# Values in per-head tile order in DRAM, rotary tables one unit earlier, gated output per head: a hybrid attention and retention block on one core

## The chip, the cores and the metric

The kernel runs on one core of a Trainium2 chip. The metric is the device time of one execution in microseconds. Five engines work side by side: TensorE (PE, with its weight loads PEld), VectorE (DVE), ScalarE (ACT), GpSimd (POOL) and SyncE (SP). Each takes its instructions in program order and waits on semaphores. Here SP issues nearly all loads and ACT nearly all stores.

## The reference

One layer over 2048 latent tokens (a grid of 32 rows by 64 columns) and 256 context tokens, width 1024, all in float32:

```
h   = rmsnorm(x) * (1 + scale) + shift          # scale, shift, gate from silu(c) @ w_ada + b_ada
na_q, na_k, na_v, na_g, r_q, r_k, r_v, r_g = split(h @ w_in)      # 8 parts of 512 columns
# group A: 8 heads of 64; each query sees a clamped 8 x 16 window of the grid and all context keys
p    = softmax([q.k_window / 8 + bias, q.k_ctx / 8])
y_na = (p @ [v_window, v_ctx]) * silu(na_g)
# group B: 4 heads of 128; rotary on q and k; retention forward and backward in chunks of 128
y_ret = head_rmsnorm(o_fwd + o_bwd) * silu(r_g)
out  = rmsnorm(x + gate * (concat(y_na, y_ret) @ w_out))
```

## The kernel before

Each float32 operand of a large product is split into a high and a low part, and a product takes three matrix multiplications (high by high, low by high, high by low). The program is one straight list of instructions in four parts.

**Preparation, 0 to 280 us.** The adaLN vectors, the normalised input in blocks of 512 tokens, the projection of the NA keys, the first units of the NA values.

**The job list, to 525 us** (`run_jobs`, L536). Twelve jobs, j0 to j11, each one group of 256 columns of w_in: j0 and j2 the NA values (9 units each, written to `vS`, 4 heads a group), j1 and j3 the retention keys of the context (one unit each), j4 and j6 the NA gates (8 units each, `gS`), j5 and j7 the retention values of the context (one unit each, `rvS`), j8 and j9 the retention gates (8 units each, `ggS`), j10 and j11 the NA queries (8 units each; the last four stand in the attention). A unit is 24 to 48 matrix multiplications into one of six PSUM buffers (`tform` L351, `tokform` L362); then ACT evacuates it (L395 a gate, L459 a retention value), and one unit later ACT's queue stores it (L143). At the start of job j, `next_w` lets ACT split the weights of job j+1 into high (L330) and low (POOL or DVE, L332), and then SP requests the weights of job j+2 (L169) into a ring of four `st` tiles. All of that stands in ACT's one queue: a split, then the job's evacuations.

Hooks hang between the units of j8 to j10. The adaLN gate row is built there: eight rows of `w_ada` come one after the other into one buffer `wraw` (L563, SP), DVE adds each, scaled, to `gacc` (L566), and the next load waits for that; `wo_row` sums `gacc` over the partitions on PE (L573) behind the second unit of j9, and ACT copies it back. Then eight rows of `w_out` go through the same buffer: DVE multiplies by the gate (L577), ACT casts (L581), POOL subtracts (L582), ACT's queue stores the parts to `woS` (L584), and the next row is loaded.

**Attention, 525 to 1085 us.** 128 tiles (8 heads, 4 query row blocks i, 4 column blocks j) run as a software pipeline over PE, DVE, ACT and POOL: scores, minimum, exponent, normalisation, transposes, product with the values (`pv`), combination. The value window of column block j has 24 or 32 columns (`CWIN`), and a row group is four grid rows, so the values of a tile lie on 96 or 128 partitions. `load_v` (L711 to L716) brings one row group with four loads from `vS`, each of 96 or 128 rows of 512 bytes. `combine` writes the head pair's result into one tile of 128 partitions, and after the odd head POOL multiplies it with the gate (L825) and one store follows. Between the tiles' matrix multiplications the fill stream places the remaining projections, among them the retention keys and queries, whose units request their rotary tables (`t0`, two buffers) in their own middle (`mid`, L405 and L435).

**Retention and output, to 1419 us.** Chunk states, retention, output projection, final norm.

The tile framework gives every DMA of SP and ACT one of eight semaphores, and a DMA waits until the one before it on its semaphore has landed, whichever of the two queues that was in. Which one it gets is fixed when the program is built.

Of the kernel before, what the change touches and what calls it, by code (L numbers as in the profile page):

```python
# [18 lines left out]
P = 128  # L19
# [51 lines left out]
]  # L71
RTYPE = [0, 1, 1, 2]
CTYPE = [0, 1, 1, 2]

# [2 lines left out]
def hybrid_kernel(ctx: ExitStack, tc: tile.TileContext, a: dict, out: bass.AP):  # L77
# [4 lines left out]
    qS = [dram.tile([4, P, 2, 512], F32, name=f"qS{t}") for t in range(4)]  # L82
    kS = [dram.tile([P, 2, LT], F32, name=f"kS{t}") for t in range(4)]
    vS = [dram.tile([LT, 4, P], F32, name=f"vS{t}") for t in range(2)]
    gS = [dram.tile([P, L], F32, name=f"gS{t}") for t in range(4)]
    rqS = [dram.tile([P, L], F32, name=f"rqS{r}") for r in range(RH)]
    rkS = [dram.tile([LT, 2 * P], F32, name=f"rkS{r}") for r in range(2)]
# [121 lines left out]
        rbs[i] = r  # L209

    def spread_copy(i):
        rbs[i, 1] = op.tile([P, 2, P], F32, name="t0")
        nc.vector.tensor_copy(rbs[i, 1], rbs[i].unsqueeze(2).to_broadcast([P, 2, P]))

    def spread(*ii):
# [149 lines left out]
                    yield  # L365
        return pm

    def mid(g, n, fn):
        for m in range(KC):
            next(g)  # L370
            if m == n:
                fn()
            yield
        return (yield from g)
# [23 lines left out]

    rot = {}

    def u_rq(w, c0, ct, b):
        def load():
            for key in ("rot_c", "rot_s"):
                rot[key] = op.tile([P, 512], F32, name="t0")
                nc.sync.dma_start(rot[key], a[key][:, b * 512:(b + 1) * 512])  # L405

        g = tform(w, ct, b)
        pm, n, tok = yield from mid(g, 3, load) if ct == 0 else g
        rc, rs = rot["rot_c"], rot["rot_s"]
# [20 lines left out]
        store(dstt[(c0 % 512) // WG][tp * 256:(tp + 1) * 256, :].rearrange("(t p) d -> p t d", p=P), r, n)  # L430

    def u_rk(w, c0, tp):
        def load():
            rot["k"] = op.tile([P, 2, 2, P], F32, name="t0")
            nc.sync.dma_start(rot["k"], a["rot_k"][tp * 256:(tp + 1) * 256].rearrange("(t p) s d -> p t s d", p=P))  # L435

        g = tokform(w, tp)
        pm = yield from mid(g, 2, load) if tp < 8 else g
        rt = rot.get("k")
# [88 lines left out]
    env["queue"] = nc.scalar  # L528
    spill = [(b, hl, k) for b in (2, 3) for hl in range(2) for k in range(0, KC, 2)]

    def spill_step():
        if spill:
            b, hl, k = spill.pop(0)
            nc.sync.dma_start(hS[b - 2][hl][:, k * 512:(k + 2) * 512], f(blk[b][hl])[:, k:k + 2, :].rearrange("p k t -> p (k t)"))

    def run_jobs(jobs, w, hooks):  # L536
        for j, (c0, units) in enumerate(jobs):
            last = j + 1 == len(jobs)
            wn = next_w(not last)
# [87 lines left out]
    def fill_stream(w):  # L627
# [63 lines left out]
    def load_head(h):  # L691
# [6 lines left out]
        return dict(k2=k2, vh=vh, vc=vc, vt={}, q={})  # L698

    def load_e(hd, h):  # L700
        hd["e"] = kp.tile([P, 16, 32], F32, name="rpbe", bufs=1)
# [9 lines left out]
    def load_v(hd, gs):  # L711
        for g in gs:
            vt = kp.tile([P, 4, P], F32R, name="vt", bufs=6)
            src = hd["vh"][4 * g * GW:(4 * g + 4) * GW, :].rearrange("(r c) d -> r c d", c=GW)
            for j, (c0, cw) in enumerate(CWIN):
                nc.sync.dma_start(f(vt)[:4 * cw, j, :], src[:, c0:c0 + cw, :])  # L716
            hd["vt"][g] = vt

    mrow = mp.tile([P, 3, 16], F32, name="mrow")
# [70 lines left out]
    def pv(t):  # L790
        h, i, j, kr0, kr, kc0, cw = dims(t)
        T, hd = tl_st[t], heads[h]
        pt, ng_, cn = T["pt"], T["ng"], 4 * cw
        if t % 2 == 0:
            tl_st["po"] = psc.tile([P, 2, 2, P], F32, name="po")
        po = tl_st["po"]
        for g in range(ng_):
            nc.tensor.matmul(po[:, t % 2, :, :], hd["vt"][kr0 // 4 + g][:cn, j, :], pt[:cn, g, :, :], start=(g == 0), stop=False)  # L798
# [4 lines left out]
    gts = {}  # L803

    def load_gate(t):
        h, i = dims(t)[:2]
        gts[t // 4] = ap_.tile([P, 512], F32, name="gt", bufs=1)
        nc.sync.dma_start(gts[t // 4], gS[h // 2][:, i * 512:(i + 1) * 512])

    def combine(t):  # L810
        h, i, j = dims(t)[:3]
        po, jp = tl_st["po"], j // 2
        fin = slice(0, 64) if h % 2 == 0 else slice(64, 128)
        oth = slice(64, 128) if h % 2 == 0 else slice(0, 64)
        if h % 2 == 0 and jp == 0:
            ys[i] = ap_.tile([P, 512], F32, name="y2", bufs=4)
# [3 lines left out]
        yv = ys[i][fin].rearrange("p (r w c) -> p w r c", r=8, w=4)[:, 2 * jp:2 * jp + 2]  # L820
        nc.vector.tensor_tensor(yv, po[fin, :, 1, :].rearrange("p j (r c) -> p j r c", r=8),
                                tmp[fin].rearrange("p j (r c) -> p j r c", r=8), ALU.add)
        if h % 2 == 1 and jp == 1:
            gt, y2 = gts.pop(t // 4), ys[i]
            nc.gpsimd.tensor_tensor(y2, y2, gt, ALU.mult)  # L825
            y_put(h // 2, i // 2, (i % 2) * 512, y2, 2)

    def run(n):
        for un in qu[n:n + 1]:
# [127 lines left out]
    for t in range(NT + 3):  # L957
# [391 lines left out]
```

## Time and profile before

| what | value |
|---|---|
| median of 3 runs | 1419.95 us (1419.73 to 1425.41) |
| the profiled execution | 1420.85 us, span 1419.1 us |
| PE busy | 1351.0 us, 95% of the span |
| mean granted TensorE clock | 0.986 |
| value loads (L716) | 256, of 64 or 48 KB |
| DMA traffic | 253.19 MB, mean 178 GB/s |

The span is the time from the first to the last instruction in the trace. A group's row gives busy time, mean length, and the idle time of the engine ahead of it with what ended it. A row of the timeline gives start, length, engine, line, operation, and in brackets the idle time ahead and its releaser. SPq and ACTq are the two engines' DMA issues.

### The profile page before, as it was taken

The numbers are of one execution on the slowest core, as the hardware profiler recorded it, in microseconds if no ns is written. First come the engines' busy times: TensorE is split into PE (matmuls) and PEld (weight loads), VectorE is DVE, ScalarE is ACT, GpSimd is POOL, SyncE is SP. The second block draws the span as 40 slices with busy tenths as digits, with TensorE's granted clock in tenths as the row PEclk, the third lists the DMA queues.
The fourth block names the chain that finished last, engine by engine and source line by source line (L and its number), as shares of the span: only waits on it lengthen the run. The fifth ranks groups of instructions, "written<-read, shape, count | busy, mean of one in ns | idle before, by whom it ended". The sixth has DMA issues, their size and how long they took to land.

```text
span 1419.1 us, 22560 instructions
## 1 busy us (share of the span) xinstructions
PE 1351.0 (95%) x8380; PEld 1181.2 (83%) x8380; DVE 641.2 (45%) x1244; ACT 530.7 (37%) x1155; POOL 560.1 (39%) x579
## 2 busy tenths in 40 slices
PE   6989999999999999999999998898999989999997
PEld 2567899988887887998799888797999879888886
DVE  5786111100021221467766766575663634345445
ACT  5454212212212221555455444354562234333332
POOL 4442302112201221565655644375453155454442
PEclk9999999999999999999999999999999999999999
DMA  9444656223254676556666685757346998555433
GB/s 318 158 164 143 215 207 230 104 97 105 96 157 159 195 276 202 127 156 166 180 157 162 182 243 190 200 153 181 108 125 208 283 297 260 191 170 173 154 120 126
DMA packets 203631, 253.19 MB, mean 178 GB/s; under 512 B 13057, under 2 KB 151425, under 8 KB 202498
## 3 DMA queue, kind: packets, MB, share of 16 engines
q1 hardware_dynamic: 168098, 186.98, 45.2%
q10 hardware_dynamic: 35424, 64.76, 12.5%
q8 instruction: 67, 1.10, 0.3%
q14 instruction: 42, 0.34, 0.1%
HBM read 168.86 MB, written 82.84 MB: 177 GB/s over the span
## 4 chain that ended last, share of the span: by engine, by line
PE 73%; DMA 9%; DVE 6%; issue 3%; POOL 3%; ACT 2%; SPq 2%; DVEq 0%; POOLq 0%; ACTq 0%
PE mm L351 25%; PE mm L362 18%; PE mm L1192 11%; PE sS L751 3%; PE tr L778 2%; PE po L798 2%; PE mm L915 2%; DMA k<-kS 2%; PE tr L780 1%; DMA q<-qS 1%; PE po L800 1%; PE mm L295 1%; PE mm L1104 1%; PE mm L1103 1%; PE mm L1102 1%
## 5 line engine op out<-in xcount | busy, mean ns | idle before, releaser
L351 PE MATMUL mm<-hhi,whi 128*128 128x512 f32 x640 | 260.5, 407 | 0.0
L351 PE MATMUL mm<-hlo,whi 128*128 128x512 f32 x640 | 254.2, 397 | 4.8 <-DVE hlo L264 1.9
L351 PE MATMUL mm<-hhi,wlo 128*128 128x512 f32 x640 | 254.4, 397 | 0.2 <-DVE wlo L332 0.2
L362 PE MATMUL mm<-whi,hhi 128*128 128x256 f32 x768 | 225.5, 294 | 0.0
L362 PE MATMUL mm<-wlo,hhi 128*128 128x256 f32 x768 | 217.7, 283 | 2.5 <-POOL wlo L332 2.5
L362 PE MATMUL mm<-whi,hlo 128*128 128x256 f32 x768 | 217.2, 283 | 0.0
L332 POOL TENSOR_TENSOR wlo<-st,whi 128x256 fp32r<-128x256 f32 (+1 forms) x97 | 111.7, 1171 | 232.7 <-ACT whi L330 232.2
L782 ACT CAST pt<-tr 128x640 fp32r<-128x640 f32 (+1 forms) x128 | 95.6, 747 | 205.4 <-PE tr L780 193.0
L788 DVE TENSOR_TENSOR pt<-tr,pt 128x640 fp32r<-128x640 f32 (+1 forms) x128 | 113.9, 890 | 102.8 <-ACT pt L782 102.1
L362 PEld LDWEIGHTS mm<-wlo,hhi 128*128 128x128 f32 x768 | 146.0, 190 | 3.2 <-POOL wlo L332 3.1
L351 PEld LDWEIGHTS mm<-hlo,whi 128*128 128x128 f32 x640 | 121.4, 190 | 30.1 <-issue 2.5
L362 PEld LDWEIGHTS mm<-whi,hhi 128*128 128x128 f32 x768 | 146.3, 190 | 0.0
L362 PEld LDWEIGHTS mm<-whi,hlo 128*128 128x128 f32 x768 | 146.2, 190 | 0.0
L351 PEld LDWEIGHTS mm<-hhi,wlo 128*128 128x128 f32 x640 | 121.0, 189 | 29.4 <-DVE wlo L332 0.6
L351 PEld LDWEIGHTS mm<-hhi,whi 128*128 128x128 f32 x640 | 121.3, 190 | 28.7 <-issue 4.6
L771 POOL TENSOR_SCALAR sp<-sp,stt 128x640 f32<-128x640 f32 (+2 forms) x128 | 103.4, 809 | 100.7 <-DVE stt L770 79.8
L760 DVE CUSTOM_DVE_ANT_0 sp<-sS,nb 128x640 f32<-128x640 f32 (+2 forms) x128 | 105.5, 825 | 26.4 <-PE sS L751 20.3
L765 ACT ACTIVATE sp<-sp,stt 128x640 f32<-128x640 f32 (+2 forms) x128 | 107.4, 839 | 26.5 <-DVE stt L760 26.0
L751 PE MATMUL sS<-k,q 128*128 128x256 f32 (+3 forms) x512 | 100.6, 319 | 16.9 <-DVE stt L760 13.0
L751 PEld LDWEIGHTS sS<-k,q 128*128 128x128 f32 x512 | 84.5, 191 | 24.4 <-DVE stt L760 15.9
L1192 PE MATMUL mm<-wor,y 128*128 128x512 f32 x384 | 95.4, 397 | 1.0 <-DVE xt L1201 0.9
L1192 PE MATMUL mm<-won,y 128*128 128x512 f32 x336 | 89.9, 406 | 0.0
(216 smaller groups left out, 2307.5 us busy)
## 6 DMA issues: line engine op xcount, KB each, us to landing
st<-in_w_in_dram SPq DMA_DIRECT2D x48, 512.0 KB
q<-qS SPq DMA_DIRECT2D x64, 256.0 KB
vS<-o ACTq DMA_DIRECT2D x18, 512.0 KB
k<-kS SPq DMA_DIRECT2D x16, 576.0 KB
kS<-o SPq DMA_DIRECT2D x16, 512.0 KB
woS<-g ACTq DMA_DIRECT2D x32, 256.0 KB
qS<-o ACTq DMA_DIRECT2D x16, 512.0 KB
vt<-vS SPq DMA_DIRECT2D x128, 64.0 KB
```

The costliest lines, as they stand in the source:

```text
L332: eng.tensor_tensor(l, r, f(h), ALU.subtract)
L351: nc.tensor.matmul(pm[:, :n], ww[:, k, cs], h[:, k, :], start=(k == 0 and i == 0), stop=(k == KC - 1 and i == 2))
L362: nc.tensor.matmul(pm[:, t * WG:(t + 1) * WG], h[:, k, o:o + P], ww[:, k, :], start=(k == 0 and i == 0), stop=(k == KC - 1 and i == 2))
L751: nc.tensor.matmul(o, hd["q"][i][:, hl, j * P:(j + 1) * P], k, start=(hl == 0), stop=(hl == 1))
L760: nc.vector.tensor_tensor_reduce(T["sp"][:, :n], T["s"], nbz[big][:, o:o + n], 1.0, 3e38, ALU.add, ALU.min, T["st"][:, 0:1])
L765: nc.scalar.activation(sp[:, :n], sp[:, :n], AF.Exp, bias=st[:, 0:1], scale=-1.0, accum_out=st[:, 1:2])
L771: nc.gpsimd.tensor_scalar(sp[:, :n], sp[:, :n], st[:, 2:3], 0.0, ALU.mult, ALU.add)
L778: nc.tensor.transpose(tr[:cn, g, :], sp[:, T["lo"] + g * cn:T["lo"] + (g + 1) * cn], ident)
L782: nc.scalar.copy(pt[:, :ng_ + 2, 0, :], tr[:, :ng_ + 2, :])
L788: nc.vector.tensor_tensor(pt[:, :n, 1, :], tr[:, :n, :], f(pt)[:, :n, 0, :], ALU.subtract)
L798: nc.tensor.matmul(po[:, t % 2, :, :], hd["vt"][kr0 // 4 + g][:cn, j, :], pt[:cn, g, :, :], start=(g == 0), stop=False)
L1192: nc.tensor.matmul(pm, yy[:, k, :], ww[:, k, sl], start=(k == 0 and i == 0), stop=(k == 3 and i == 2))
```

## The change

Four edits:

1. A new DRAM tile `vB` per head holds the values in the order in which attention's tiles read them: [row in the tile, row group, window, feature]. 256 copies from `vS` to `vB`, DRAM to DRAM, of 64 or 48 KB (four grid rows by 24 or 32 columns by 512 bytes), are issued on SP, six behind each unit of jobs j4 and on.
2. `load_v` takes two loads per row group from `vB`, of 128 and 96 rows of 1 KB. The windows' order in the tile is `VORD`. Row groups 3 and 4 are requested one tile earlier.
3. The rotary tables are requested in the middle of the unit ahead, from three `t0` buffers; `mid` goes.
4. Gate, product and store run per head on 64 partitions, with two buffers each for gate and result: 32 products on POOL and 32 stores in place of 16.

```diff
+VORD = [1, 2, 0, 3]
...
+    vB = [dram.tile([P, 8, 4, P], F32, name=f"vB{h}") for h in range(NH)]
...
+    def rot_load(key, n):
+        rot[key, n] = t = op.tile([P, 512], F32, name="t0", bufs=3)
+        if key == "rot_k":
+            nc.sync.dma_start(t.rearrange("p (t s d) -> p t s d", t=2, s=2),
+                              a[key][n * 256:(n + 1) * 256].rearrange("(t p) s d -> p t s d", p=P))
+        else:
+            nc.sync.dma_start(t, a[key][:, n * 512:(n + 1) * 512])
+
     def u_rq(w, c0, ct, b):
-        def load():
-            for key in ("rot_c", "rot_s"):
-                rot[key] = op.tile([P, 512], F32, name="t0")
-                nc.sync.dma_start(rot[key], a[key][:, b * 512:(b + 1) * 512])
-
-        g = tform(w, ct, b)
-        pm, n, tok = yield from mid(g, 3, load) if ct == 0 else g
-        rc, rs = rot["rot_c"], rot["rot_s"]
+        pm, n, tok = yield from tform(w, ct, b)
+        rc, rs = rot["rot_c", b], rot["rot_s", b]
...
+    vfmt = []
+    for h in range(NH):
+        vg = vS[h // 4][:L, h % 4, :].rearrange("(r c) d -> r c d", c=GW)
+        for e, j in enumerate(VORD):
+            c0, cw = CWIN[j]
+            for g in range(8):
+                vfmt.append((vB[h][:4 * cw, g, e, :].rearrange("(r c) d -> r c d", c=cw), vg[4 * g:4 * g + 4, c0:c0 + cw, :]))
...
                 tick()
                 spill_step()
+                for _ in range(6 if j > 3 else 0):
+                    if vfmt:
+                        nc.sync.dma_start(*vfmt.pop(0))
                 if hooks.get(j):
                     hooks[j].pop(0)()
...
         def steps(g):
-            for v in g:
+            n = at[0]
+            at[0] += 1
+            short = n > 0 and order[n - 1][0] is u_rq
+            if short:
+                for e in needs(n)[1:]:
+                    rot_load(*e)
+            held = order[n][0] is u_rq
+            for m, v in enumerate(g):
+                if m == 2:
+                    nxt = needs(n + 1)
+                    for e in nxt[:1] if held else nxt:
+                        rot_load(*e)
                 if chop:
                     chop.pop(0)()
                 yield v
...
     def load_v(hd, gs):
         for g in gs:
             vt = kp.tile([P, 4, P], F32R, name="vt", bufs=6)
-            src = hd["vh"][4 * g * GW:(4 * g + 4) * GW, :].rearrange("(r c) d -> r c d", c=GW)
-            for j, (c0, cw) in enumerate(CWIN):
-                nc.sync.dma_start(f(vt)[:4 * cw, j, :], src[:, c0:c0 + cw, :])
+            for e, n in ((0, P), (2, 96)):
+                nc.sync.dma_start(f(vt)[:n, e:e + 2, :], hd["vb"][:n, g, e:e + 2, :])
...
-        if h % 2 == 1 and jp == 1:
-            gt, y2 = gts.pop(t // 4), ys[i]
-            nc.gpsimd.tensor_tensor(y2, y2, gt, ALU.mult)
-            y_put(h // 2, i // 2, (i % 2) * 512, y2, 2)
+        if jp == 1:
+            gt = gts.pop(t // 4)
+            nc.gpsimd.tensor_tensor(y2[fin], y2[fin], gt[fin], ALU.mult)
+            store(yS[i // 2][h // 2, fin, (i % 2) * 512:(i % 2) * 512 + 512], y2[fin], 2)
...
-        if h % 2 == 1 and j == 3:
+        if j == 1:
             load_gate(t)
...
-        for g in {(0, 3): (3,), (1, 0): (4,), (1, 1): (5,), (1, 3): (6,), (2, 3): (7,)}.get((i, j), ()):
+        for g in {(0, 2): (3,), (0, 3): (4,), (1, 1): (5,), (1, 3): (6,), (2, 3): (7,)}.get((i, j), ()):
             load_v(hd, (g,))
```

PE and DVE run the same instructions in the same order as before. SP's order changes at three places.

SP in j4 to j9 of the changed program (L546 the copies, L171 the weights' loads, L565 the loads of the gate chain's rows), rows alike in a run put together:

```order
L546 DMA vB_67<-vS_65 128x1x128 x16
L546 DMA vB_67<-vS_65 96x1x128 x16
L546 DMA vB_68<-vS_65 128x1x128 x16
L171 DMA st<-in_w_in_dram 128x4x256 x2
L546 DMA vB_68<-vS_65 96x1x128 x6
L171 DMA st<-in_w_in_dram 128x4x256 x2
L546 DMA vB_68<-vS_65 96x1x128 x10
L546 DMA vB_69<-vS_65 128x1x128 x16
L546 DMA vB_69<-vS_65 96x1x128 x16
L546 DMA vB_70<-vS_65 128x1x128 x6
L171 DMA st<-in_w_in_dram 128x4x256 x2
```

In the program before these weights' loads follow each other with nothing between. Now j4's 48 copies stand ahead of the weights of j7 (the first row of L171), six more ahead of those of j8, and j6's 48 ahead of those of j9. The 16th copy of j4 has its semaphore from the store of j5's unit (`rvS0<-o`), the ninth of j6 from the store of j7's unit (`rvS1<-o`).

ACT at the start of j6 in the changed program (L450 and L145 j5's evacuation and store, L332 the split of j7's weights, L389 and L145 the first evacuations and stores of j6):

```order
L450 COPY o_2742<-mm_2693 128x512 [waits DMAHW4_49,PE_49]
L145 DMA rvS0_85<-o_2742 128x2x256 [waits Activation_49]
L332 CAST whi_2751<-st_2689 128x1024 [waits DMAHW1_49,Pool_49]
L332 CAST whi_2751<-st_2691 128x1024 [waits DMAHW2_49]
L389 ACTIVATE o_2786<-mm_2761 128x512 [waits DMAHW6_49,PE_49]
L145 DMA gS2_77<-o_2786 128x512 [waits DMAHW4_49,Activation_49]
```

ACT's order is that of before; what moved is the load of `st_2689`, which now stands behind 48 copies on SP, the sixteenth of which waits for the second row here.

SP at the gate chain, before:

```order
L169 DMA st_2993<-in_w_in_dram 128x4x256 [waits DMAHW3_49,DMAHW0_49,Pool_49]
L558 DMA gacc_3027<-in_b_gate_dram 1x1024 [waits DMAHW2_49,DVE_49]
L563 DMA wraw_3030<-in_w_ada_dram 128x1024 [waits DMAHW3_49]
L563 DMA wraw_3061<-in_w_ada_dram 128x1024 [waits DMAHW5_49,DMAHW3_49,DVE_49]
L563 DMA wraw_3092<-in_w_ada_dram 128x1024 [waits DMAHW7_49,DMAHW5_49,DVE_49]
```

and in the changed program:

```order
L560 DMA gacc_3149<-in_b_gate_dram 1x1024 [waits DMAHW6_49,DVE_49]
L565 DMA wraw_3152<-in_w_ada_dram 128x1024 [waits DMAHW7_49]
L546 DMA vB3_70<-vS0_65 96x1x128 [waits DMAHW0_49]
L546 DMA vB3_70<-vS0_65 96x1x128 [waits DMAHW1_49]
L546 DMA vB3_70<-vS0_65 96x1x128 [waits DMAHW2_49]
L546 DMA vB3_70<-vS0_65 96x1x128 [waits DMAHW3_49]
L546 DMA vB3_70<-vS0_65 96x1x128 [waits DMAHW4_49]
L546 DMA vB3_70<-vS0_65 96x1x128 [waits DMAHW5_49]
L565 DMA wraw_3189<-in_w_ada_dram 128x1024 [waits DMAHW7_49,DMAHW6_49,DVE_49]
```

Six copies stand between every two loads of the chain. The first load's semaphore (DMAHW7) was last given to the store of j9's unit 0, `ggS2<-o_3448`, and that of the copy behind it (DMAHW0) to the store of j9's unit 1, `ggS2<-o_3485`; the unit that needs the sum of all eight rows, `wo_row`, stands behind unit 1 on PE.

More of the change, by code (lines that the diff above doesn't have):

```diff
@@ L211, in spread_copy @@
     def spread_copy(i):
-        rbs[i, 1] = op.tile([P, 2, P], F32, name="t0")
+        rbs[i, 1] = op.tile([P, 2, P], F32, name="t0", bufs=3)
         nc.vector.tensor_copy(rbs[i, 1], rbs[i].unsqueeze(2).to_broadcast([P, 2, P]))
@@ L366, in tokform @@
         return pm
[L368 to L374, printed above, removed]
     def u_k(w, c0, ct, b):
@@ L432, in u_rk @@
     def u_rk(w, c0, tp):
[L433 to L439, printed above, removed]
+        pm = yield from tokform(w, tp)
+        rt = rot["rot_k", tp].rearrange("p (t s d) -> p t s d", t=2, s=2) if tp < 8 else None
         o = op.tile([P, 2, 2, WG], F32, name="o")
@@ L642, in next_c, with needs @@
             return w
-        def steps(g):
-            for v in g:
+        order = [(kind, *a_) for kind, c0 in fseq[:4] for b in range(2) for a_ in units(kind, b)]
+        order += [(kind, *a_) for b in range(4) for kind, c0 in fseq[4:6] for a_ in units(kind, b)]
+        order += [(kind, *a_) for kind, c0 in fseq[6:] for b in (2, 3) for a_ in units(kind, b)]
+        at = [0]
+        def needs(n):
+            kind, *a_ = order[n] if n < len(order) else (None,)
+            if kind is u_rk:
+                return [("rot_k", a_[0])]
+            if kind is u_rq and a_[0] == 0:
+                return [("rot_c", a_[1]), ("rot_s", a_[1])]
+            return []
+        def steps(g):
+            n = at[0]
[10 more added lines that the diff above has]
+                        rot_load(*e)
                 if chop:
@@ L697, in load_head @@
         nc.sync.dma_start(f(vc), vh[L:, :].rearrange("(n p) d -> p n d", p=P))
-        return dict(k2=k2, vh=vh, vc=vc, vt={}, q={})
+        return dict(k2=k2, vb=vB[h], vc=vc, vt={}, q={})
     def load_e(hd, h):
@@ L792, in pv @@
         T, hd = tl_st[t], heads[h]
-        pt, ng_, cn = T["pt"], T["ng"], 4 * cw
+        pt, ng_ = T["pt"], T["ng"]
         if t % 2 == 0:
@@ L796, in pv @@
         po = tl_st["po"]
+        cn = 4 * cw
         for g in range(ng_):
-            nc.tensor.matmul(po[:, t % 2, :, :], hd["vt"][kr0 // 4 + g][:cn, j, :], pt[:cn, g, :, :], start=(g == 0), stop=False)
+            nc.tensor.matmul(po[:, t % 2, :, :], hd["vt"][kr0 // 4 + g][:cn, VORD.index(j), :], pt[:cn, g, :, :], start=(g == 0), stop=False)
         for g in range(2):
@@ L803, in hybrid_kernel, with fin_ @@
     gts = {}
+    def fin_(h):
+        return slice(0, 64) if h % 2 == 0 else slice(64, 128)
     def load_gate(t):
         h, i = dims(t)[:2]
-        gts[t // 4] = ap_.tile([P, 512], F32, name="gt", bufs=1)
-        nc.sync.dma_start(gts[t // 4], gS[h // 2][:, i * 512:(i + 1) * 512])
+        gts[t // 4] = ap_.tile([P, 512], F32, name="gt", bufs=2)
+        nc.sync.dma_start(gts[t // 4][fin_(h)], gS[h // 2][fin_(h), i * 512:(i + 1) * 512])
     def combine(t):
@@ L812, in combine @@
         po, jp = tl_st["po"], j // 2
[L813 to L816, printed above, removed]
+        fin, oth = fin_(h), fin_(h + 1)
+        if jp == 0:
+            ys[i] = ap_.tile([P, 512], F32, name="y2", bufs=2)
+        y2 = ys[i]
         tmp = ap_.tile([P, 2, P], F32, name="cmb", bufs=1)
```

2 lines of the change are left out of this document (1 added, 1 removed).

## The prediction

> **What bounds the kernel now.** I read the page first (busy time by engine), then the window table by stage, then the waits of SP's queue, then the timelines of SP, ACT, DVE and PE where the new copies stand.
>
> ```profile
> PE 1351.0 (95%) x8380; PEld 1181.2 (83%) x8380; DVE 641.2 (45%) x1244; ACT 530.7 (37%) x1155; POOL 560.1 (39%) x579
> 280.00:525.00 245.00, 245.00 (x1098) 198.91 (x1097) 32.05 (x29) 50.47 (x77) 47.24 (x29) 1.00 0.46 153
> 525.00:1085.00 560.00, 528.17 (x3813) 494.85 (x3812) 333.97 (x744) 270.40 (x567) 298.64 (x344) 0.98 0.61 170
> ```
>
> The window rows give the stretch, its length, the busy time of PE, PEld, DVE, ACT and POOL, PE's granted clock, the DMA engines' busy share and GB/s. PE bounds the kernel. In the job list (280 to 525) it never idles; there is nothing to win there, and every wait put into it lengthens the span one for one. In the attention (525 to 1085) it idles 560 − 528.17 = 31.8 us: all that the load and rotary edits can work on, with the clock lost around it.
>
> The job list is safe only because loads come early enough. These SP and ACT rows carry the weights of the sixth and eighth of its jobs, counted from zero as j6 (the NA gate, L395) and j8 (the retention gate):
>
> ```profile
> 329.66 8.46 SPq L169 DMA_DIRECT2D st<-in_w_in_dram  x4
> 380.10 2.72 SPq L169 DMA_DIRECT2D st<-in_w_in_dram  x2
> 331.40 0.38 ACTq L143 DMA_DIRECT2D rvS<-o  x1
> 331.82 2.00 ACT L330 CAST whi<-st 128x1024 fp32r<-128x1024 f32 x2 [0.45 <-ACT o L459]
> 336.36 0.60 ACT L395 ACTIVATE o<-mm 128x512 f32<-128x512 f32 x1 [2.54 <-PE mm L351]
> 341.94 0.60 ACT L395 ACTIVATE o<-mm 128x512 f32<-128x512 f32 x1 [4.99 <-PE mm L351]
> 381.83 0.38 ACTq L143 DMA_DIRECT2D rvS<-o  x1
> 386.79 0.60 ACT L395 ACTIVATE o<-mm 128x512 f32<-128x512 f32 x1 [2.54 <-PE mm L351]
> ```
>
> Each row is start, duration, engine, line. SP has the weights' loads out at 329.66, before j5's last store at 331.40; ACT splits weights (L330) and then evacuates one unit every 341.94 − 336.36 = 5.58 us, in order. A load that comes late blocks ACT at the split, and PE stops when its six PSUM buffers are full.
>
> SP's queue also waits for ACT's stores, by semaphores that DMAs of both queues share:
>
> ```profile
> SPq L716 <- DMA qS<-o: 6.1, 2, 3.8
> SPq L169 <- DMA gS<-o: 6.3, 2, 3.2
> ```
>
> (Total us, times, longest.) A q store has nothing to do with L716's value load; still the load waited up to 3.8 us for its landing. Today this is rare, since SP is ahead. The changed program puts 256 DMAs into this queue.
>
> **Price of a copy and of a store.** The trace has no DRAM-to-DRAM copy. The nearest rows are today's value loads, of the same 64 and 48 KB with the same source:
>
> ```profile
> 547.41 13.81 SPq L716 DMA_DIRECT2D vt<-vS  x12
> 579.13 2.57 SPq L716 DMA_DIRECT2D vt<-vS  x4
> 582.97 7.70 SPq L716 DMA_DIRECT2D vt<-vS  x8
> 450.14 2.26 ACTq L584 DMA_DIRECT2D woS<-g  x4
> 455.42 0.62 ACT L581 CAST g<-wraw 128x512 fp32r<-128x512 f32 x1 [0.70 <-DMA woS<-g]
> ```
>
> Per load 0.64 (2.57/4), 0.96 (7.70/8), 1.15 (13.81/12, with waits inside). I take 0.8 per copy, between issue alone and the busy row. A copy that is faster than its issue is excluded, as issue is in order. For a store, the last of the four woS was issued before 452.40 and released ACT at 455.42: 3.0 us.
>
> The Trainium skill, "DMA: Bandwidth & Descriptors", sections "Why a DMA increments its semaphore by 16 and not by 1" and "Specifications", speaks against these copies: the number of engines follows the slowest dimension of both sides, here the four grid rows of the source, so four of 16 engines work, at about 27 GiB/s each. Estimate from that page: 56 KB (a mean copy) over four engines is 0.5 us, and beside other traffic at the window's share of 0.46, 0.5/0.54 = 0.92 us per copy. The trace's row of 0.96 agrees; by 0.92 the sum below would be 8.5 us larger (71 copies on the path), about 1502.
>
> **The change, part by part.** Where SP stands in the changed program is in the order rows ahead of this; all times are from before.
>
> *j6's start.* Of j4's 48 copies the sixteenth shares its semaphore with j5's store of 331.40. So SP stands until 331.40 + 3.0 = 334.4, issues 32 more copies (× 0.8 = 25.6) and only then the loads of j7's weights, at 360.0. A 512 KB load takes about 4.0 (from the gate chain below: cycle 5.26 less 1.28). ACT's split (2.00) and its next evacuation (0.60) end at 366.6. PE needs that evacuation at 336.36 + 5 × 5.58 = 364.3. Stall 2.3 (0 at 0.64; 13.5 at 1.15). The six copies of j5 stand the same way on j6's stores, ahead of j8's weights, so their low half comes late to PE: 2 (0 to 5).
>
> *j8's start.* j6's copies: the ninth stands on the store of 381.83, 39 follow. 381.83 + 3.0 + 31.2 = 416.0, and 6.6 as above: 422.6, where PE needs 386.79 + 5 × 5.58 = 414.7. Stall 7.9 (1.7 at 0.64; 21.6 at 1.15).
>
> *The adaLN gate row.* The largest term. Eight rows of w_ada go one after the other through one buffer: load, DVE product (L566), next load; PE then sums them in wo_row (L573).
>
> ```profile
> 383.33 38.46 SPq L563 DMA_DIRECT2D wraw<-in_w_ada_dram  x8
> 432.20 0.33 ACTq L143 DMA_DIRECT2D ggS<-o  x1
> 437.80 0.33 ACTq L143 DMA_DIRECT2D ggS<-o  x1
> 388.57 1.28 DVE L566 SCALAR_TENSOR_TENSOR gacc<-wraw,silc,gacc 128x1024 f32<-128x1024 f32 x1 [6.12 <-DMA wraw<-in_w_ada_dram]
> 420.15 1.28 DVE L566 SCALAR_TENSOR_TENSOR gacc<-wraw,silc,gacc 128x1024 f32<-128x1024 f32 x1 [4.64 <-DMA wraw<-in_w_ada_dram]
> 430.35 1.28 DVE L566 SCALAR_TENSOR_TENSOR gacc<-wraw,silc,gacc 128x1024 f32<-128x1024 f32 x1
> 436.97 1.88 PE L573 MATMUL mm<-gacc,one 128*128 128x512 f32 x4
> ```
>
> Today the chain starts at 383.33 and its last product ends at 430.35 + 1.28 = 431.6, 5.3 us ahead of wo_row. In the changed program its first load waits for the store of j9's unit 0 (432.20), and a copy ahead of the second load waits for that of unit 1 (437.80). wo_row stands right behind unit 1 on PE, and needs all eight. So second load: 437.80 + 3.0 + six copies by issue (× 0.64 = 3.8) = 444.6. Six more cycles of 5.26 ((420.15 − 388.57)/6) to 6.9 (six copies of 1.15 do not fit into the load's time); I take 5.6: 478.2. Load and product 5.3: 483.5. PE waits 483.5 − 436.97 = 46.5 (44.5 to 54.3). Nothing covers it: PE's units behind wo_row stand in program order, j9's and j10's.
>
> *The scaled output weights.* The w_out rows go through the same buffer during j9 and j10.
>
> ```profile
> 448.75 45.45 SPq L563 DMA_DIRECT2D wraw<-in_w_out_dram  x6
> 503.32 0.34 SPq L563 DMA_DIRECT2D wraw<-in_w_out_dram  x1
> 452.44 0.83 ACTq L143 DMA_DIRECT2D ggS<-o  x1
> 508.00 1.23 DVE L577 TENSOR_TENSOR wraw<-wraw,gacc 128x1024 f32<-128x1024 f32 x1 [5.59 <-DMA wraw<-in_w_out_dram]
> 510.92 0.69 DVE L389 TENSOR_TENSOR o<-mm,o 128x512 fp32r<-128x512 f32 x1 [1.69 <-ACT o L388]
> 517.08 0.40 PE L351 MATMUL mm<-hhi,whi 128*128 128x512 f32 x1
> ```
>
> Twelve copies now stand between the first and second of these loads, one of them behind the ggS store of 452.44: 455.4, two more copies, 457.0 against 448.75, so 8.3 late. Each of six later cycles has six copies, some of them behind the cycle's own stores; between 0.6 and 3.0 late each, 2 taken: 12. The DVE evacuation behind the last product ends at 511.6, and PE wants that buffer at 517.08: 5.5 of cover. 8.3 + 12 − 5.5 = 14.8 (6.4 to 20.8).
>
> *The last 46 copies* stand behind the last w_out load and ahead of the attention's: 37 us, where 547.41 − 503.32 = 44.1, less the 5.5 just used, is room. Nothing; at 1.15, 14.
>
> *Attention.* Half as many value loads, tables one unit earlier, per-head gates.
>
> ```profile
> 905.00:920.00 15.00, 8.45 (x45) 7.04 (x44) 6.24 (x13) 3.06 (x6) 3.93 (x4) 0.77 0.75 188
> 978.00:993.00 15.00, 10.46 (x71) 10.26 (x70) 4.96 (x12) 6.65 (x16) 10.19 (x13) 0.77 0.64 183
> 838.00:862.00 24.00, 17.65 (x92) 14.86 (x91) 11.55 (x25) 7.23 (x14) 9.50 (x11) 0.86 0.75 186
> ```
> ```profile
> 898.95 4.56 DMA vt<-vS
> ...
> 903.60 8.46 DMA t<-in_rot_s_dram
> ...
> 915.19 1.65 PE sS L751 x4
> ```
> ```profile
> L825 POOL TENSOR_TENSOR y<-y,gt 128x512 f32<-128x512 f32 x16 | 20.7, 1291 | 44.5 <-DVE y L821 44.5
> ```
>
> The chain of waits at 903.60 to 915.19 is a sine table that stands behind value loads: this stall, 15 − 8.45 = 6.55, and the clock behind it, (1 − 0.77) × 15 = 3.45, go: 10. Of the other two (4.54 and 6.35 idle, 3.45 and 3.4 of clock) 17.7 could go at most; their chains run over k, q and weight loads, which stay, so 5. Against it, 16 more POOL products (same length, since half the partitions: 16 × 1.29 = 20.7 on POOL, busy 299 of 560) and 16 more stores: 3. Sum −12 (−28 to +5).
>
> *Clock.* The last three windows show some 3.4 us lost after a longer stall. Three new long ones (j8, gate row, w_out), and half of that for the two short: 12 (8 to 15).
>
> **Sum:** 2.3 + 2 + 7.9 + 46.5 + 14.8 + 0 − 12 + 12 = 73.5 on the span of 1419.1: 1492.6. Around the span lie 1420.85 − 1419.1 = 1.75, and the median of the runs is 0.9 below the profiled execution: 1493.5, so 1494.
>
> **Rivals.** *The copies stay hidden* (other side): SP's waits on the late stores end sooner than PE needs, because SP runs ahead of ACT; the attention's gain is all that is left, −12 to −28: about 1400. For it: SP is idle most of the job list. Against it: the gate row, where two stores are named in the program and stand one unit ahead of PE's need; it decides only if the first gate load goes out before 432. 5%. *The gate chain does not bind,* but the rest does: without 46.5 and its clock, 1444. For it: the waits could be met by other DMAs; against it, the same rows. 7%. *Copies at 1.15 or more:* j6 +11.2, j8 +13.7, gate +7.8, w_out +6, low half +3: 1535, and 1549 with the last copies' 14. For it: the 13.81 row, and DMA at 0.46 before the copies; against it, that row has waits inside. 17%. That the load edits bring nothing would be 1511, within the forecast's own.
>
> **How the numbers follow.** Forecast 71%, with its own bounds on cycles, copies and attention about 1465 to 1520. To hold 8 in 10 the range goes down to the gate rival's side (1450) and up into the slow copies (1545). A measurement of this kernel tells 0.5% (7 us) from no change. Slower takes the forecast, the gate rival and the slow copies, 95%; of the hidden-copies 5%, 4 are faster, 1 the same.
>
> **What would show it.** A PE wait of 40 us or more ahead of wo_row with DVE's gate product as releaser; the first wraw load issued right after j9's first ggS store landed; ACT idle ahead of its splits at j6 and j8 on st; about 20 copies in 13 to 23 us where nothing waits; no stall on a rotary table in the attention. PE busy throughout the job list would make the prediction wrong; so would a first gate load before j9, or copies above 1.2 us each.

## The result, and the profile after

The changed kernel takes 1526.07 us (median of 4 runs, 1524.18 to 1527.11) against 1422.68 for the kernel before: ratio 1.0725, 95% interval 1.0692 to 1.0758. The prediction was 1494, with a range of 1450 to 1545. The profiled execution has a span of 1525.2 us, 106.1 more than before.

The window tables below cut both spans at the attention's first score (561.9 before, 686.8 after) and at the first chunk state of the retention (1077.0 and 1182.0). Columns as in the prediction: stretch, length, busy time of PE, PEld, DVE, ACT, POOL, granted clock, DMA share, GB/s. Before:

```profile
0.00:561.90 561.90, 539.84 (x2845) 439.71 (x2846) 157.61 (x237) 153.17 (x240) 138.25 (x98) 1.00 0.52 176
561.90:1077.00 515.10, 483.31 (x3589) 457.32 (x3587) 325.19 (x726) 261.67 (x548) 282.82 (x324) 0.97 0.61 166
1077.00:1419.00 342.00, 327.88 (x1948) 284.13 (x1948) 158.40 (x281) 115.85 (x368) 139.00 (x157) 0.99 0.63 200
```

After:

```profile
0.00:686.80 686.80, 549.58 (x2845) 444.72 (x2845) 157.05 (x238) 155.51 (x243) 135.50 (x96) 0.92 0.50 166
686.80:1182.00 495.20, 478.14 (x3588) 452.40 (x3588) 324.61 (x725) 259.63 (x545) 305.15 (x343) 0.99 0.62 171
1182.00:1525.00 343.00, 326.38 (x1948) 283.49 (x1948) 158.43 (x281) 115.83 (x368) 139.22 (x157) 0.99 0.64 201
```

Ahead of the attention the kernel lost 124.9 us: PE does the same 2845 matrix multiplications, is busy 9.7 us longer (the clock), and idles 137.2 in place of 22.1. The attention itself became 19.9 us shorter. What follows it is 1.0 longer.

Where PE waited, from the table of its waits (total us, times, longest):

```profile
PE mm L575 <- issue: 50.0, 1, 50.0
PE sS L776 <- DMA q<-qS: 38.6, 1, 38.6
PE mm L353 <- DVE o L383: 16.2, 2, 8.5
PE mm L353 <- ACT o L389: 7.2, 2, 3.9
```

L575 is `wo_row`, L776 the attention's first score, L353 the units of j8 to j10. "issue" at the first row is no releaser: the wait ends at 494.87, 0.1 us behind the last product of the gate chain (493.48 + 1.28), as the timelines of DVE and PE show:

```profile
493.48 1.28 DVE L568 SCALAR_TENSOR_TENSOR gacc<-wraw,silc,gacc 128x1024 f32<-128x1024 f32 x1 [2.83 <-DMA wraw<-in_w_ada_dram]
494.87 3.75 PE L575 MATMUL mm<-gacc,one 128*128 128x512 f32 x4 [50.03 <-issue]
```

So the row that names the longest wait of the program does not name its cause; the neighbour in time does.

What held SP, from 280 to 700 us, in the table of its queue's waits:

```profile
SPq L546 <- DMA gS<-o: 47.8, 12, 10.0
SPq L546 <- DMA qS<-o: 46.7, 9, 7.0
...
SPq L546 <- DMA woS<-g: 32.0, 10, 10.0
SPq L546 <- DMA ggS<-o: 23.3, 7, 7.4
...
SPq L546 <- DMA vB<-vS: 4.8, 8, 1.7
```

L546 is the copies' line. They read `vS` and write `vB`, and wait 149.8 us (47.8 + 46.7 + 32.0 + 23.3) for stores of the gates, the queries and the output weights, which touch neither. For one another's landing they wait 4.8 us.

And SP's timeline at the places of the prediction:

```profile
283.13 72.35 SPq L546 DMA_DIRECT2D vB<-vS  x48
355.58 1.34 SPq L171 DMA_DIRECT2D st<-in_w_in_dram  x2
...
444.41 0.36 SPq L565 DMA_DIRECT2D wraw<-in_w_ada_dram  x1
448.91 3.81 SPq L546 DMA_DIRECT2D vB<-vS  x6
452.83 0.40 SPq L565 DMA_DIRECT2D wraw<-in_w_ada_dram  x1
...
488.41 0.34 SPq L565 DMA_DIRECT2D wraw<-in_w_ada_dram  x1
...
593.45 77.36 SPq L546 DMA_DIRECT2D vB<-vS  x46
670.91 1.13 SPq L171 DMA_DIRECT2D st<-in_w_in_dram  x2
```

The first gate load goes out at 444.41 in place of 383.33, the eighth at 488.41. The last row pair is what the prediction did not see: the 46 copies behind the last w_out load took 77 us, and the attention's loads stand behind them.

### The profile page after: what moved, and what is told of

Read it like the earlier page. It is cut to its first block, busy times and chain, and to the rows that moved or that the text cites. A ratio compares the mean times of both kernels' runs of the same rounds, so it can differ in the third digit from the quotient of the medians.

```text
span 1525.2 us, 22857 instructions
## 1 busy us (share of the span) xinstructions
PE 1354.1 (89%) x8380; PEld 1180.6 (77%) x8380; DVE 640.1 (42%) x1244; ACT 531.0 (35%) x1155; POOL 579.9 (38%) x595
## 4 chain that ended last, share of the span: by engine, by line
PE 58%; DMA 11%; issue 10%; DVE 6%; SPq 6%; POOL 5%; ACT 3%; ACTq 0%; POOLq 0%; DVEq 0%
PE mm L364 15%; PE mm L353 15%; PE mm L1221 10%; SPq L546 5%; PE sS L776 3%; PE tr L803 2%; PE po L824 2%; PE mm L944 2%; POOL wlo L334 1%; PE tr L805 1%; DMA v<-rvS 1%; PE po L826 1%; PE mm L297 1%; POOL sp L796 1%; DMA gS<-o 1%
## 5 line engine op out<-in xcount | busy, mean ns | idle before, releaser
L353 PE MATMUL mm<-hhi,whi 128*128 128x512 f32 x640 | 263.9, 412 | 23.3 <-DVE o L383 16.2
L353 PE MATMUL mm<-hlo,whi 128*128 128x512 f32 x640 | 256.4, 401 | 3.9 <-DVE hlo L266 2.3
L353 PE MATMUL mm<-hhi,wlo 128*128 128x512 f32 x640 | 256.5, 401 | 1.7 <-POOL wlo L334 1.7
L353 PEld LDWEIGHTS mm<-hhi,whi 128*128 128x128 f32 x640 | 123.2, 192 | 54.4 <-DVE o L383 17.1
L353 PEld LDWEIGHTS mm<-hhi,wlo 128*128 128x128 f32 x640 | 122.3, 191 | 31.4 <-POOL wlo L334 2.1
L353 PEld LDWEIGHTS mm<-hlo,whi 128*128 128x128 f32 x640 | 123.0, 192 | 30.3 <-issue 3.5
L776 PE MATMUL sS<-k,q 128*128 128x256 f32 (+3 forms) x512 | 99.0, 315 | 41.2 <-DMA q<-qS 38.6
L776 PEld LDWEIGHTS sS<-k,q 128*128 128x128 f32 x512 | 83.8, 190 | 47.8 <-DMA q<-qS 39.1
## 6 DMA issues: line engine op xcount, KB each, us to landing
k<-kS SPq DMA_DIRECT2D x16, 576.0 KB
```

The lines of the kernel that those rows point to most:

```text
L353: nc.tensor.matmul(pm[:, :n], ww[:, k, cs], h[:, k, :], start=(k == 0 and i == 0), stop=(k == KC - 1 and i == 2))
L776: nc.tensor.matmul(o, hd["q"][i][:, hl, j * P:(j + 1) * P], k, start=(hl == 0), stop=(hl == 1))
```

## The experiments

The theory after the result: the copies cost what they cost because of where they stand in SP's queue and with which ACT stores they share a semaphore; their bytes cost little; and the attention's gain is the rotary tables' and the loads'. Rivals: the bytes; the 256 issues in one queue, whatever they wait for; a loss in the other edits. Each ratio below is to the kernel before, timed together with that run (medians 1421.96 to 1422.99 us).

### The change without its copies

```diff
-                for _ in range(6 if j > 3 else 0):
-                    if vfmt:
-                        nc.sync.dma_start(*vfmt.pop(0))
...
-            for e, n in ((0, P), (2, 96)):
-                nc.sync.dma_start(f(vt)[:n, e:e + 2, :], hd["vb"][:n, g, e:e + 2, :])
+            src = hd["vh"][4 * g * GW:(4 * g + 4) * GW, :].rearrange("(r c) d -> r c d", c=GW)
+            for j, (c0, cw) in enumerate(CWIN):
+                nc.sync.dma_start(f(vt)[:4 * cw, VORD.index(j), :], src[:, c0:c0 + cw, :])
```

> The change without its copies: no vB, four value loads from vS as before; rotary tables one unit earlier, row groups 3 and 4 one tile earlier, gate, product and store per head stay. Theory: the copies in SP's queue are the whole loss, and most of the 20 us that the attention won comes from the rotary tables, so 1400 to 1408 us, with no PE wait over 4 us between 280 and 560. Rival (the per-head products and stores, or the table loads, cost something that the copies hide): 1415 or more. Rival (the attention's gain is that of the two loads per row group): about 1418, with the stall on the sine table back.

1422.88 us, ratio 1.0003 (0.9989 to 1.0017). The loss is gone with the copies, and so is most of the gain. The window of its attention:

```profile
561.80:1074.20 512.40, 480.30 (x3589) 453.28 (x3587) 324.83 (x726) 262.15 (x548) 303.34 (x340) 0.98 0.62 167
```

PE idles 32.1 us there, as before (31.8). The scores' waits on DVE, the sine table's stall among them, did shrink, but time came back at query loads. The scores' two rows in the table of PE's waits, before and in this run:

```profile
PE sS L751 <- DVE stt L760: 13.0, 7, 6.6
PE sS L751 <- DMA q<-qS: 3.6, 1, 3.6
```
```profile
PE sS L765 <- DVE stt L774: 3.4, 5, 1.0
PE sS L765 <- DMA q<-qS: 8.1, 3, 4.7
```

The chain of waits around one of them:

```profile
842.29 11.81 DMA rkS<-o
...
854.70 5.82 DMA q<-qS
...
860.65 1.25 PE sS L765 x4
```

The query load (L722) waited for a store of the retention keys, and SP's timeline has four value loads in 8.05 us just ahead of it. Taking one late load out of a full queue made the next one late. My theory on the tables fell. By its time the run fits both rivals; the runs with the two loads alone, below, bear out the second, that the gain is theirs, though the stall on the sine table that it expected did not come back.

### The copies alone

Before, with `vB`, the list of copies and the issuing loop, nothing reading `vB`.

> Before with the 256 copies alone (on SP, six behind each unit from j4 on; nobody reads them). Theory: all of the loss ahead of the attention, 125 us, is there: 1535 to 1550, with the wait of about 50 us ahead of the gate row's sum, some 20 us in the w_out rows and some 38 us at the attention's first scores. Rival (part of the loss comes from the new loads or tables): under 1525.

1541.78 us, ratio 1.0842 (1.0816 to 1.0867). As the theory had it: the whole loss comes with the copies. The first score comes at 686.5, as in the change (686.8). PE's longest waits are the same two:

```profile
PE mm L586 <- issue: 48.6, 1, 48.6
PE sS L764 <- DMA q<-qS: 41.0, 2, 38.9
```

### The copies cut to 4 KB

Of each copy's rows of 24 or 32 columns only two columns are copied (nothing reads `vB` in this kernel):

```diff
-vB[h][:4 * cw, g, e, :].rearrange("(r c) d -> r c d", c=cw), vg[4 * g:4 * g + 4, c0:c0 + cw, :]
+vB[h][:4 * cw, g, e, :].rearrange("(r c) d -> r c d", c=cw)[:, 0:2, :], vg[4 * g:4 * g + 4, c0:c0 + 2, :]
```

> As the run with the copies alone, each copy cut to two columns (4 KB in place of 64 or 48): the same number at the same places of SP's queue. In this built program the first gate load shares its semaphore with j7's store, not with j9's, and no copy ahead of the second one stands behind a store of j9. Theory (what costs is which late ACT stores SP's loads share a semaphore with): the wait ahead of the gate row goes, 1418 to 1440. Rival (256 issues of 0.6 us in SP's one queue are enough): over 1480. Bytes as the cause would also be fast here; the run with the copies on GpSimd's queue tells that apart.

1425.82 us, ratio 1.0023 (1.0004 to 1.0043). 256 issues at the same places of SP's queue, each of 0.56 us in the median (0.59 in the change), cost 3 us. The rival on the issues falls; bytes and semaphores changed together here.

### The copies on GpSimd's queue

```diff
-                        nc.sync.dma_start(*vfmt.pop(0))
+                        nc.gpsimd.dma_start(*vfmt.pop(0))
```

> The whole change, its 256 copies of full size issued on GpSimd's queue in place of SP's; their semaphores are others than those that SP and ACT share. Theory (order and shared semaphores): SP's weight and gate loads are as early as before, no wait of 50 us ahead of the gate row's sum; 1395 to 1425, unless POOL's own queue is held up by the issues (then its subtractions of the weights are late, and PE waits for wlo). Rival (the bytes, DRAM to DRAM beside the other traffic): stays above 1480.

1415.17 us, ratio 0.9946 (0.9926 to 0.9967). All bytes move, at nearly the same time of the program, and nearly all of the loss is gone. The rival on the bytes falls. The first score still comes at 576.0 in place of 561.9, 10.0 us of it a wait on the query load. Part of that is the theory's own caveat: the last copies stand ahead of POOL's weight subtraction, and SP's load of weights at 547.74 waits for it. What ends last is the shared semaphore again, with no copy left in SP's queue. The loads behind 547.74 wait for one query store after another, as the end of the chain ahead of the first score shows:

```profile
567.43 2.68 DMA qS<-o
...
570.13 0.33 SPq L728
...
571.00 5.00 DMA q<-qS
```

L728 loads a table of the attention's bias; the query's load stands behind it.

### The copies walked column first

```diff
-vB[h][:4 * cw, g, e, :].rearrange("(r c) d -> r c d", c=cw), vg[4 * g:4 * g + 4, c0:c0 + cw, :]
+vB[h][:4 * cw, g, e, :].rearrange("(r c) d -> c r d", c=cw), vg[4 * g:4 * g + 4, c0:c0 + cw, :].rearrange("r c d -> c r d")
```

> The whole change with one line edited: both sides of each copy are walked column first, so the slowest dimension is 24 or 32 columns in place of four rows. Same 256 copies, same bytes, same rows of 512 bytes, same places in SP's queue. In this built program the semaphores fall otherwise: the first gate load and the copies up to the second share theirs with other copies and not with the ggS stores of j9, and j4's and j6's copies with earlier ones too. Theory (the loss is which ACT stores SP's DMAs share a semaphore with): the 50 us ahead of the gate row's sum goes, and most of the 38 at the attention's start; 1400 to 1430. Rival (256 full-size copies in SP's one queue cost what they cost, wherever the semaphores fall): over 1480. The Trainium skill, "DMA: Bandwidth & Descriptors", section "Why a DMA increments its semaphore by 16 and not by 1": more engines per copy, which by itself would shorten a copy's landing, not its issue; at 0.64 us per issue that alone is worth little here.

1417.38 us, ratio 0.9964 (0.9943 to 0.9985). Same copies, same bytes, same places in SP's queue, and 109 us less than the change. SP's waits and its timeline in this kernel:

```profile
SPq L546 <- DMA ggS<-o: 12.7, 6, 3.2
...
SPq L546 <- DMA gS<-o: 8.3, 2, 4.6
...
SPq L546 <- DMA woS<-g: 4.3, 2, 3.0
```
```profile
283.72 35.25 SPq L546 DMA_DIRECT2D vB<-vS  x48
...
388.19 0.36 SPq L565 DMA_DIRECT2D wraw<-in_w_ada_dram  x1
...
515.00 41.34 SPq L546 DMA_DIRECT2D vB<-vS  x46
```

The copies now wait 25.3 us for ACT's stores in place of 149.8. A copy's issue did not get cheaper (35.25/48 = 0.73 us, where the narrow ones run at 0.64 when nothing holds them). What differs is the order in which the built program hands out the eight semaphores: the DMA ahead of the first gate load on its semaphore is now another copy, issued at 383.43, and was j9's store of 439.90. About as many copies as in the change stand behind a store on their semaphore, but behind earlier ones: in the change the last 46 copies stand behind query stores up to the sixteenth, here up to the seventh. That the builder judges narrow copies slower, and therefore plans them among later stores, is my reading of the two programs and is not shown by a run. The rows show that the waits on ACT's stores went and the time with them. By the Trainium skill's rule on engines per copy ("DMA: Bandwidth & Descriptors", "Why a DMA increments its semaphore by 16 and not by 1") these copies use more engines than the narrow ones. No run here measures that or a shorter landing; the copies' waits on one another's landing could have given at most the 4.8 us of the change.

Not all is won back: the first score comes at 573.8, 11.9 us later than before, and the attention's 497.3 us make up for it.

### Copies for three heads

The list of copies stops after 96; heads 3 to 7 load from `vS` with four loads.

```diff
-    for h in range(NH):
+    for h in range(3):
         vg = vS[h // 4][:L, h % 4, :].rearrange("(r c) d -> r c d", c=GW)
```

> The whole change with copies for the first three heads alone (96 copies, narrow as in the change, six behind each unit of j4 to j6), whose values come with two loads; the other five heads' with four loads from vS. No copy in j8 to j11, so the gate chain's, the w_out rows' and the attention's first loads follow each other in SP's queue as before; j4's 48 copies and their semaphores are as in the change. Theory (each stall belongs to the copies that stand at its place): ahead of the attention only the stalls of j6 to j8 stay, together under 8 us, none at the gate row; the first scores at 562 to 572; 1412 to 1430. Rival (copies early in the queue push everything behind them): over 1460.

One run, 1450.69 us. Neither side had it. The stalls at the w_out rows and at the attention's start are gone, but 19.5 us are left at the gate row, with no copy between its loads:

```profile
PE mm L575 <- issue: 19.5, 1, 19.5
```
```profile
376.87 33.30 SPq L546 DMA_DIRECT2D vB<-vS  x42
...
413.05 32.56 SPq L565 DMA_DIRECT2D wraw<-in_w_ada_dram  x6
```

The copies of j4 to j6 put the chain's start from 383.33 to 413.05, and its 5.3 us of cover cannot take that. If this holds for the change too, some 20 of its 50.0 us come of copies ahead of the chain, and some 30 of those inside it with j9's stores.

### Values stored straight into the per-head order

No copies; each unit of j0 and j2 stores its tile into `vB` itself, 16 stores on ACT's queue, once with the rest of the change and once with the two loads alone.

```diff
-        store(vS[(c0 - 1024) // WG][tp * 256:(tp + 1) * 256].rearrange("(t p) h d -> p t (h d)", p=P),
-              f(vt).rearrange("p t h e d -> p t (h e d)"))
+        for e, j in enumerate(VORD):
+            w0, cw = CWIN[j]
+            dst = vB[(c0 - 1024) // WG][:, :4 * cw, tp, e, :].rearrange("h (r c) d -> r c h d", c=cw)
+            for r in range(4):
+                store(dst[r], f(vt)[64 * (r % 2) + w0:64 * (r % 2) + w0 + cw, r // 2].rearrange("p h e d -> p (h e) d"))
```

> The whole change without copies: each unit of the value jobs j0 and j2 stores its tile straight into the per-head order, with 16 stores on ACT's queue in place of one into vS (the context's unit still goes to vS). Everything of the attention as in the change. Theory (the attention's 20 us are real and the copies' place is the loss): 1396 to 1406, attention about 495 from the first scores to the first chunk state, before it as in the kernel before (562). Rival (16 stores a unit on ACT hold up its evacuations in j0 and j2): a PE wait there, 1410 or more.

> Before with the values stored straight into the per-head order and the two loads per row group (row groups 3 and 4 one tile earlier); rotary tables and the gate and product of a head pair as before. Theory (the gain is that of two loads in place of four, since the change without the copies gained nothing): 1398 to 1408. Rival (the two loads gain only together with the earlier tables): 1410 to 1420, with a stall of 4 us or more on the sine table left.

1478.03 us (1.0395, 1.0361 to 1.0429) and 1476.29 (1.0381, 1.0345 to 1.0416): the rival of the first was right, and the second missed both of its ranges, by the same wait. ACT stands in its own queue; its timeline in the first of the two, one unit in a steady stretch, and PE's waits:

```profile
217.24 0.37 ACT L420 CAST o<-mm 128x256 fp32r<-128x256 f32 x1 [7.82 <-DMA vB<-o]
...
218.96 8.11 ACTq L145 DMA_DIRECT2D vB<-o  x16
227.12 0.37 ACT L420 CAST o<-mm 128x256 fp32r<-128x256 f32 x1 [8.64 <-DMA vB<-o]
```
```profile
PE mm L364 <- ACT whi L332: 34.7, 1, 34.7
PE mm L353 <- ACT whi L332: 32.4, 1, 32.4
```

This unit takes ACT 227.12 − 217.24 = 9.9 us, those behind it 9.0, and the next job's weight split stands behind the last of nine. What these two runs tell on the attention is clean, since it starts behind all that. Its windows, of the first and of the second:

```profile
637.20:1132.00 494.80, 475.45 (x3590) 449.23 (x3588) 324.99 (x726) 262.11 (x548) 302.97 (x340) 1.00 0.62 171
```
```profile
635.10:1129.90 494.80, 475.75 (x3589) 450.51 (x3587) 324.98 (x726) 261.84 (x548) 282.97 (x324) 1.00 0.62 172
```

494.8 us in both. The two loads per row group are the attention's whole gain; beside them, earlier tables and per-head gates add nothing to it.

### Gate, product and store per head alone

No copies, rotary tables as before, row groups 3 and 4 one tile earlier.

```diff
-    def rot_load(key, n):
...
+        g = tform(w, ct, b)
+        pm, n, tok = yield from mid(g, 3, load) if ct == 0 else g
```

> The change without copies and without the earlier rotary tables: gate, product and store per head, four value loads from vS, row groups 3 and 4 one tile earlier. The run without the copies lasted 4 to 5 us longer behind the attention than before. Theory (this comes of the 32 stores and products per head): again 346 us from the first chunk state to the end, 1420 to 1428 with the stall on the sine table. Rival (it comes of the tables): 342 there, 1417 to 1421.

1429.09 us, ratio 1.0044 (1.0026 to 1.0062), 0.4% slower, and above both ranges. Behind the attention it takes 342.0 us, so the 4 us that the run without the copies had lost there do not come of the per-head stores alone. They go with the tables: the six kernels here with the earlier tables take 343.2 to 347.0 us behind the attention, the seven without them 340.3 to 342.2. No run has the tables alone, and by what they cost stays open. The time is lost in the attention, which takes 523.2 us here, with PE idle for 39.0; the three kernels of this document whose attention is that of before take 512.6 to 518.9, and the run with the earlier tables added 512.4. So with four value loads the per-head gates and stores seem not to be free.

### The two loads with column-first copies

Before with the copies walked column first and two loads per row group; tables and gates as before.

> Before with the 256 copies walked column first (as in the run on the whole change with that edit) and two loads per row group; rotary tables and the gates of a head pair as before. Theory (the two loads are the whole gain, the tables and the per-head gates bring nothing): equal to the whole change with the column-first copies within 0.4%, 1408 to 1418, attention 493 to 500 and 342 us behind it. Rival (the tables matter once the copies are out of the way): 1424 or more.

1416.36 us, ratio 0.9949 (0.9926 to 0.9972), against 0.9964 (0.9943 to 0.9985) for the whole change with such copies: the same. Its profiled execution was the longest of ten (span 1422.7), with 501.7 us for the attention, just above what was expected, and 341.9 behind it. Over all the kernels of this document, the attention takes 493.3 to 501.7 us in the seven where every head has two loads, and 512.4 to 523.2 in the five where every head has four.

### Eight stores of 2 KB, on two queues

The run with straight stores and the two loads alone (the second of two above), but with the heads inside a row of `vB`, so that one store takes all four heads and both halves of a unit: 8 stores in place of 16, four on ACT's queue and four on GpSimd's. Loads as two per row group, of 512 byte rows.

```diff
+            dst = vB[(c0 - 1024) // WG][:4 * cw, tp, e].rearrange("(t r c) h d -> r c t (h d)", t=2, r=2)
+            for r in range(2):
+                src = f(vt)[64 * r + w0:64 * r + w0 + cw].rearrange("p t h e d -> p t (h e d)")
+                q = nc.gpsimd if e > 1 else env["queue"]
+                defer(1, lambda q=q, d=dst[r], s=src: q.dma_start(d, s))
```

> Before with the values stored straight into the per-head order, heads inside a row, so that a unit of the value jobs needs 8 stores of 2 KB rows in place of 16: the four of 32 columns on ACT's queue, the four of 24 on GpSimd's; two loads per row group, of 512 byte rows; tables and gates as before. The 16 stores held ACT 9.0 us per unit where PE needs some 5.6. Theory: four stores are 1.8 us, ACT keeps up, no stall in j0 to j2; the attention as with two loads, about 495; 1396 to 1406, below both kernels. Rival (the gain of the two loads is that of the 1 KB rows): attention 505 or more, 1410 to 1420.

1407.94 us, ratio 0.9892 (0.9863 to 0.9921): 1.1% less than the kernel before, and 2 us above the range expected. No stall in the value jobs is left above 1.4 us. Its windows:

```profile
0.00:566.40 566.40, 542.64 (x2844) 440.35 (x2845) 157.45 (x237) 152.80 (x240) 175.73 (x162) 0.99 0.58 187
566.40:1064.30 497.90, 475.35 (x3589) 450.33 (x3588) 325.15 (x726) 261.68 (x548) 282.89 (x324) 1.00 0.63 171
```

The rival on the 1 KB rows falls: with 512 byte rows the attention takes 497.9 us, inside the 493.3 to 501.7 of the runs with 1 KB rows, and 17 fewer than before with four loads.

## Why the prediction was right, step by step

The direction, the place and most of the size held; one term was missed altogether. The measured 1526 lies above the forecast's own bounds (1465 to 1520). It is inside the range only by the room that was left for slow copies, and the copies were not slow: that part is luck.

| step | predicted | measured |
|---|---|---|
| j6's start | 2.3 | 0 |
| low half of j8's weights | 2 | 1.7 |
| j8's start | 7.9 | 3.9 |
| gate row | 46.5 | 50.0 |
| w_out rows | 14.8 | 19.4 (3.2, 8.5 and 7.7) |
| last 46 copies | 0 | 38.6 |
| clock ahead of the attention | 12 | 9.7 |
| attention, with its clock | −12 | −19.9 |
| sum on the span | 73.5 | 106.1 (with 2.7 of small waits and behind the attention) |

*Price of a copy.* 0.8 was taken, with 0.92 and 1.15 beside it; where nothing held them the copies went out at 0.64 to 0.74. In j4, the copy that had waited for j5's store and the 32 behind it went out from 333.54 to 355.58, 0.67 each. That, and a store that lands in 2.2 us rather than 3.0 (issued 331.37, the copy behind it 333.54), made the two early stalls smaller than predicted. The step itself was right: the sixteenth copy went out right behind that store, and ACT stood 29.4 us ahead of j6's split and 34.8 ahead of j8's for the weights.

*The gate row* went as written: first load behind j9's first store, second behind the store of unit 1, then six cycles of (488.41 − 452.83)/6 = 5.93 us where 5.6 was taken. The run with three heads adds what the prediction did not say: with no copy in the chain at all, 19.5 us stayed.

*The last 46 copies* is the step that failed. The prediction gave them 37 us by their issue and let 38.6 us of room hide them. They took 77.36, because they waited for the query stores of j10 and j11, 39.9 us in this stretch, the last wait among them:

```profile
649.50 2.61 DMA qS<-o
652.13 0.59 SPq L546
```

This is from the chain of waits after: behind the last query store's landing 28 copies still had to go out. The mechanism is the one that the prediction used at the gate row, and it was not carried on to the stretch where nothing seemed to need SP. With column-first copies the same 46 took 41.34 us, close to the 37, and PE came to its first score at 573.77 without a wait.

*The attention* gained more than said, for another reason. The stalls were read right in the trace before (a table behind value loads), but the remedy was credited to the earlier tables. The run without the two loads and with the tables keeps PE's idle time there (32.1 us); the run with only the two loads brings it to 494.8 − 475.75 = 19.1. What counted were the value loads ahead of the late one.

*The rivals.* The hidden copies, and the gate chain that does not bind (1444), fell with the 50.0 us at the gate row. The slow copies (1535) came near the time for the wrong reason: copies were faster than 0.8, and the missing 38.6 stood elsewhere. That the load edits bring nothing would be 1506 by the prediction's own sum; its 1511 takes the upper bound of +5.

## What to carry to other kernels

A load on an idle queue is cheap only as long as the queue stays ahead: before a few hundred transfers go into it, list for every later load on it what it will wait for, also through semaphores that DMAs of another queue share, and carry that to the end of the stretch. A longest wait with no releaser named is read from the neighbouring engine's last row. When several loads are late in turn, fewer transfers ahead of them helps where requesting one of them earlier moves the stall to the next.

## What the runs showed of the hardware that was not expected

Copies from DRAM to DRAM of 48 to 64 KB go out every 0.64 to 0.74 us on SP where nothing holds them, and on GpSimd's queue every 0.67 (48 in 32.02 us). There all 256 of them, beside the job list's other traffic, put the first score back by no more than 14.1 us. And one edit that changes neither the bytes nor SP's order, the dimension that is walked first, moved the kernel by 109 us, while the copies' waits for ACT's stores went from 149.8 us to 25.3.
